# A hybrid decoder layer: the first three chunks side by side, and ten k-tiles of x transposed by blocks and a trip through DRAM

## The chip, the cores and the metric

The kernel runs on one core of a Trainium2 chip. The metric is the device time of one execution in microseconds. A core has five engines that work side by side, each with a queue of its own: TensorE (PE; its weight loads are shown as PEld), VectorE (DVE), ScalarE (ACT), GpSimd (POOL) and SyncE (SP), which here issues nearly all DMAs. An engine does its instructions in the order in which they stand; one that waits holds up all behind it.

## What is computed

One layer on x of 256 tokens by 2048, in float32: RMS-norm, one combined projection, two attention mixers, gates, an output projection, and an MLP.

```python
h = rms_norm(x, g_mix)
proj = h @ w_in                      # 2048 -> 11776: q, k, v of 12 + 8 heads, two gates
...                                  # dilated attention (12 heads), MoBA attention (8 heads)
mixed = jax.nn.sigmoid(g_a) * ya + jax.nn.sigmoid(g_b) * yb
x = x + mixed @ w_out
h2 = rms_norm(x, g_mlp)
x = x + jnp.square(jax.nn.relu(h2 @ w_up)) @ w_down
```

Here only the beginning matters: x is transposed, scaled by g_mix, and multiplied with w_in.

## The kernel before

**Slots.** All the large products are written as one list of 496 slots. A slot multiplies two k-tiles (2 x 128 rows) of a weight matrix, 512 columns wide (a chunk), with the 256 tokens. Float32 is done as three products of halves: `split` makes hi (ScalarE casts, line 150) and lo (VectorE subtracts, line 151) of the weights, and `split_tr` does the same for the transposed activations (lines 160, 161). A slot is 12 matmuls of 512 columns (lines 176 to 178): two k-tiles, two halves of the tokens, three products. w_in has 23 chunks of 8 slots each; before, chunk after chunk. A chunk's result is in two PSUM banks of tag acc, of which there are four.

**The loop.** At the end of the kernel a loop over j writes the program: the splits up to slot j + 2, the loads of weight pieces (1 MB, two slots each; `raw` has three buffers, hi and lo three each), then what the tables `at_dma`, `at_post` and `at_fill` hold for j, with the matmuls of slot j ahead of `at_fill`. For the slots in `EARLY`, `at_post` comes ahead of the splits. This sets only the order within each engine's queue. What stands at slot 16 in the code is not held back until then, unless it waits for something or stands behind something that waits.

**The start.** SyncE loads x in eight pieces and the first weight pieces in turn. TensorE does some warming transposes (line 655, 661), then transposes x: `x_fill(i)` (line 232) does two k-tiles with four transposes into two banks of tag fill, `x_post(i)` scales and splits them into `xT`. `x_fill(0)` stands ahead of slot 0, the other seven in and behind slots 0 to 5. GpSimd loads small gain vectors (lines 649, 652).

**A chunk's post work.** When a q or k chunk is done in slot j, `qk_done` puts into the tables: squares at j + 1 and j + 2, the scaling to `qn` at j + 3, 32 x 32 block transposes into `tq` at j + 4 (`blk`, line 210), four scatters of `tq` to DRAM at j + 6 (`wr`, line 215), one gather back at j + 8 (`rd`, line 220), the gain at j + 11. `tq` has one buffer. A scatter and a gather together complete the transposition; SyncE issues the gather only when the scatters have landed.

Of the kernel before, what the change touches and what calls it, by code (L numbers as in the profile page):

```python
# [76 lines left out]
def hybrid_block_kernel(ctx: ExitStack, tc: tile.TileContext, x, g_mix, w_in, q_norm_a, k_norm_a,  # L77
# [86 lines left out]
    def tok_major(banks, actT, k, first, last, hi, lo, between=None, cut=False):  # L164


        parts = [(0, 0, CW), (1, 0, CW)] if not cut else [(0, 0, CW), (1, 0, S), (1, S, CW)]
        order = [(i, kk) for i in range(len(parts)) for kk in range(2)]
        if between:
            order = [(i, kk) for kk in range(2) for i in range(2)]  # L170
        for i, (n, kk) in enumerate(order):
            t, a, b = parts[n]
            o = banks[t][:, a:b]
            s_hi = actT[:, k + kk, 0, t * P:(t + 1) * P]
            s_lo = actT[:, k + kk, 1, t * P:(t + 1) * P]
            nc.tensor.matmul(o, lhsT=s_hi, rhs=hi[:, kk, a:b], start=first and kk == 0, stop=False)  # L176
            nc.tensor.matmul(o, lhsT=s_hi, rhs=lo[:, kk, a:b], start=False, stop=False)  # L177
            nc.tensor.matmul(o, lhsT=s_lo, rhs=hi[:, kk, a:b], start=False, stop=last and kk == 1 and b == CW)  # L178
            if between and i == 1:
                between()  # L180

    def tok_chunk(src, k0, nk, c0, actT, ka, done):
# [584 lines left out]
```

## Time and profile before

| | |
|---|---|
| median of 3 runs | 1394.58 us (1394.02 to 1395.3) |
| the profiled execution | 1394.08 us, its span 1392.3 us |
| TensorE busy | 1385.7 us of the span |
| VectorE, ScalarE, GpSimd busy | 805.4, 649.1, 30.0 us |
| DMA | 317.67 MB, 228 GB/s on average |
| chain that ended last | 99% TensorE, 1% DMA |

The chain that ended last is followed back from the last instruction, at each step to what released it. A row of the timeline says when an instruction started, how long it took, its engine, line and operation, what it wrote and read, and in brackets how long the engine had been idle and what ended that. Rows with x4 stand for four instructions in a row; the time is that of all.

### The profile page before, as it was taken

The numbers are of one execution on the slowest core, as the hardware profiler recorded it, in microseconds if no ns is written. First come the engines' busy times: TensorE is split into PE (matmuls) and PEld (weight loads), VectorE is DVE, ScalarE is ACT, GpSimd is POOL, SyncE is SP. The second block draws the span as 40 slices with busy tenths as digits, with TensorE's granted clock in tenths as the row PEclk, the third lists the DMA queues.
The fourth block names the chain that finished last, engine by engine and source line by source line (L and its number), as shares of the span: only waits on it lengthen the run. The fifth ranks groups of instructions, "written<-read, shape, count | busy, mean of one in ns | idle before, by whom it ended". The sixth has DMA issues, their size and how long they took to land.

```text
span 1392.3 us, 16021 instructions
## 1 busy us (share of the span) xinstructions
PE 1385.7 (100%) x6168; PEld 1148.6 (83%) x6168; DVE 805.4 (58%) x951; ACT 649.1 (47%) x924; POOL 30.0 (2%) x49
## 2 busy tenths in 40 slices
PE   9999999999999999999999999999999999999998
PEld 7888888888888888888888888888888888888887
DVE  5666546666555544776657566544445656654443
ACT  6554445454444464444545445433334544543332
POOL 1101000010000000000000000000000000000000
PEclk9999999999999999999999999999999999999999
DMA  8777986778566655777878777665567787766562
GB/s 273 234 251 223 291 269 222 241 262 271 188 212 213 219 195 185 254 257 269 275 216 259 251 237 246 213 206 185 194 198 214 228 253 235 248 214 220 202 208 95
DMA packets 193027, 317.67 MB, mean 228 GB/s; under 512 B 8360, under 2 KB 54840, under 8 KB 192952
## 3 DMA queue, kind: packets, MB, share of 16 engines
q1 hardware_dynamic: 192664, 316.65, 70.0%
q8 instruction: 48, 0.79, 0.2%
q14 instruction: 27, 0.22, 0.0%
q0 software_dynamic: 256, 0.01, 0.0%
q10 hardware_dynamic: 32, 0.01, 0.0%
HBM read 288.85 MB, written 27.79 MB: 227 GB/s over the span
## 4 chain that ended last, share of the span: by engine, by line
PE 99%; DMA 1%; SPq 0%; DVE 0%; ACT 0%; issue 0%; DVEq 0%
PE acc L178 28%; PE acc L177 28%; PE acc L176 28%; PE fill L177 4%; PE fill L176 4%; PE fill L178 4%; PE fill L395 1%; PE fill L442 1%; DMA raw<-in_w_in_dram 1%; PE fill L394 0%; PE fill L444 0%; SPq L139 0%; PE fill L232 0%; SPq L224 0%; DVE lo L151 0%; ACT hi L150 0%
## 5 line engine op out<-in xcount | busy, mean ns | idle before, releaser
L151 DVE TENSOR_TENSOR lo<-raw,hi 128x1024 fp32r<-128x1024 f32 (+1 forms) x498 | 606.2, 1219 | 565.3 <-ACT hi L150 564.2
L150 ACT CAST hi<-raw 128x1024 fp32r<-128x1024 f32 (+1 forms) x498 | 523.0, 1051 | 688.5 <-PE acc L178 576.0
L176 PE MATMUL acc<-hi,xT 128*128 128x512 f32 x736 | 289.2, 393 | 0.0
L177 PE MATMUL acc<-lo,xT 128*128 128x512 f32 x736 | 286.7, 390 | 0.4 <-DVE lo L151 0.4
L178 PE MATMUL acc<-hi,xT 128*128 128x512 f32 x736 | 286.8, 390 | 0.0
L176 PE MATMUL acc<-hi,x1T 128*128 128x512 f32 x512 | 199.2, 389 | 0.0
L177 PE MATMUL acc<-lo,x1T 128*128 128x512 f32 x512 | 199.2, 389 | 0.0
L178 PE MATMUL acc<-hi,x1T 128*128 128x512 f32 x512 | 199.2, 389 | 0.0
L177 PEld LDWEIGHTS acc<-lo,xT 128*128 128x128 f32 x736 | 138.2, 188 | 29.7 <-DVE lo L151 1.1
L178 PEld LDWEIGHTS acc<-hi,xT 128*128 128x128 f32 x736 | 138.1, 188 | 29.2 <-DVE xT L161 0.5
L176 PEld LDWEIGHTS acc<-hi,xT 128*128 128x128 f32 x736 | 138.3, 188 | 28.3
L176 PEld LDWEIGHTS acc<-hi,x1T 128*128 128x128 f32 x512 | 96.1, 188 | 20.1
L177 PEld LDWEIGHTS acc<-lo,x1T 128*128 128x128 f32 x512 | 96.1, 188 | 19.9
L178 PEld LDWEIGHTS acc<-hi,x1T 128*128 128x128 f32 x512 | 96.1, 188 | 19.9
L177 PE MATMUL fill<-lo,h 128*128 128x512 f32 (+1 forms) x258 | 99.9, 387 | 0.0
L178 PE MATMUL fill<-hi,h 128*128 128x512 f32 (+1 forms) x258 | 99.9, 387 | 0.0
L176 PE MATMUL fill<-hi,h 128*128 128x512 f32 (+1 forms) x258 | 99.9, 387 | 0.0
L176 PE MATMUL acc<-hi,h 128*128 128x512 f32 x256 | 99.6, 389 | 0.0
L177 PE MATMUL acc<-lo,h 128*128 128x512 f32 x256 | 99.6, 389 | 0.0
L178 PE MATMUL acc<-hi,h 128*128 128x512 f32 x256 | 99.6, 389 | 0.0
L176 PEld LDWEIGHTS fill<-hi,h 128*128 128x128 f32 x258 | 48.4, 188 | 10.0
L178 PEld LDWEIGHTS fill<-hi,h 128*128 128x128 f32 x258 | 48.4, 188 | 9.9
(118 smaller groups left out, 1069.1 us busy)
## 6 DMA issues: line engine op xcount, KB each, us to landing
raw<-in_w_in_dram SPq DMA_DIRECT2D x89, 1024.0 KB, 5.8
raw<-in_w_up_dram SPq DMA_DIRECT2D x64, 1024.0 KB, 5.8
raw<-in_w_down_dram SPq DMA_DIRECT2D x64, 1024.0 KB, 5.1
scr<-tq SPq DMA_DIRECT2D x136, 128.0 KB, 4.9
raw<-in_w_out_dram SPq DMA_DIRECT2D x16, 1024.0 KB, 5.4
st<-scr SPq DMA_DIRECT2D x29, 512.0 KB, 5.6
raw<-in_w_branch_b_dram SPq DMA_DIRECT2D x8, 1024.0 KB, 5.2
raw<-in_w_branch_a_dram SPq DMA_DIRECT2D x4, 1024.0 KB, 5.0
```

The source lines that it names most:

```text
L150: nc.scalar.copy(hi[:, o], t[:, o])
L151: nc.vector.tensor_tensor(lo[:, o], t[:, o], hi[:, o].bitcast(F32), op=ALU.subtract)
L176: nc.tensor.matmul(o, lhsT=s_hi, rhs=hi[:, kk, a:b], start=first and kk == 0, stop=False)
L177: nc.tensor.matmul(o, lhsT=s_hi, rhs=lo[:, kk, a:b], start=False, stop=False)
L178: nc.tensor.matmul(o, lhsT=s_lo, rhs=hi[:, kk, a:b], start=False, stop=last and kk == 1 and b == CW)
L395: nc.tensor.matmul(b[:, P:P + S], lhsT=q[:, 1], rhs=k, start=True, stop=True)
L442: nc.tensor.matmul(st["o"][:, o:o + S], lhsT=v[:, 0, h * HD:(h + 1) * HD], rhs=pt[:, 0:2], start=(g == 0 or not joint), stop=False)
```

## The change

- **Side by side.** The first 24 slots take the chunks 0, 1 and 2 in turn, two k-tiles at a time (`stream_beside`): slot 0 is chunk 0 with k-tiles 0 and 1, slot 1 chunk 1 with the same, slot 2 chunk 2, slot 3 chunk 0 with k-tiles 2 and 3. A weight piece holds two such halves and is loaded by two DMAs. Chunks 2 and 3 use banks of tag fill. Chunks 0, 1 and 2 end in slots 21, 22 and 23, and their post work is shifted by 0, 3 and 6 slots.
- **Bounces.** K-tiles 0 to 5 of x are still transposed by TensorE. K-tiles 6 to 10 and 11 to 15 go through `x_bounce`: block transposes on VectorE (slots 2 and 5), four scatters to DRAM (3 and 6), one gather (5 and 9), scaling and splitting (7 and 12). x is loaded in five pieces.
- **Order of matmuls.** In slot 0 the products go k-tile by k-tile, first those with the hi half of the weights; `split(1)` works on both k-tiles at once.
- **Small loads.** The gain loads stand at slot 16, what uses them at 26; the sums of squares of x at 9 to 15.

```diff
-EARLY = (1, 2, 3, 4, 5, 6)
+EARLY = (1, 2, 5, 7)
...
+    def stream_beside(src, nk, c0, mains):
+
+        turns = [(a, i) for a in range(0, nk, 2) for i in range(len(mains))]
+        for n in range(0, len(turns), 2):
+            aps = [(2 * h, 2 * h + 2, src[a * P:(a + 2) * P, c0 + i * CW:c0 + (i + 1) * CW].rearrange(
+                "(k p) c -> p k c", p=P)) for h, (a, i) in enumerate(turns[n:n + 2])]
+            for h, (a, i) in enumerate(turns[n:n + 2]):
+                slots.append((aps, 2 * h, a, mains[i]))
...
+        if order == "start":
+            for kk in range(2):
+                for i in (0, 2, 1):
+                    for t in range(2):
+                        product(t, kk, 0, CW, i)
+            return
...
+    def x_bounce(u, k0, n, steps):
+
+        tq = T["xs"][:, u, 0].rearrange("p (t j f) -> p t j f", t=2, j=4)
+        st = T["xs"][:, u, 1].rearrange("p (t f) -> p t f", t=2)
+        scr = dp.tile([2, 4, 32, 4, 32 * n], F32, name=f"scrx{u}")
...
+        on(at_post, steps[0], blk)
+        on(at_dma, steps[1], lambda: scatter(scr, tq))
+        on(at_dma, steps[2], lambda: gather(st, scr))
+        on(at_post, steps[3], post)
...
-    def qk_done(kind, nh_off):
+    def qk_done(kind, nh_off, later=0):
 
         def done(banks, j):
+            j += later
...
-            done = qk_done("aq" if c < 3 else "ak", 4 * c)
+            done = qk_done("aq" if c < 3 else "ak", 4 * c, (0, 3, 6)[c] if c < 3 else 0)
...
+        if c < 3:
+            beside.append(tok_main(KD, lambda: T["xT"], 0, done, "fill" if c == 2 else "acc"))
+            if c == 2:
+                stream_beside(w_in, KD, 0, beside)
+        else:
+            tok_chunk(w_in, 0, KD, c * CW, lambda: T["xT"], 0, done, "fill" if c == 3 else "acc")()
...
-    x_post(0, b0)
-    split(0)
-
-    def mid():
-        split(1)
-        x_post(1, x_fill(1))
-        split(2)
-        load_all(3)
-        x_load(7)
-
-    T["mid"] = mid
-    for i in range(2, 8):
+    x_post(0, b0, (0,))
+    split(0, lambda: x_post(0, b0, (1,)))
+    split(1)
+    for i in (1, 2):
         st = {}
-        on(at_fill, i - 2, lambda i=i, st=st: st.update(b=x_fill(i)))
-        on(at_post, i - 1, lambda i=i, st=st: x_post(i, st["b"]))
-    on(at_post, 9, gain_post)
+        on(at_fill, i - 1, lambda i=i, st=st: st.update(b=x_fill(i)))
+        on(at_post, i, lambda i=i, st=st: x_post(i, st["b"]))
+    x_bounce(0, 6, 5, (2, 3, 5, 7))
+    x_bounce(1, 11, 5, (5, 6, 9, 12))
+    on(at_post, 16, gain_load)
+    on(at_post, 26, gain_post)
```

Three places show how the order in the queues moves. In all of them the name behind "waits" is a semaphore: DMAHW is one of the eight that SyncE's loads use in turn, so waiting for it is waiting for a DMA to land; DVE, Activation and Pool are engines.

The first is GpSimd's queue at the start; `half` is a constant, `grow` and `gn` take the gains, `sx` and `rstd` belong to the norm of x. Before, it stands so:

```order
L614 MEMSET half 128x8
L647 MEMSET grow_83 128x32
L649 DMA grow_83<-in_g_mlp_dram 16x32 [waits Pool_49]
L649 DMA grow_83<-in_g_mlp_dram 16x32 x3
L652 DMA gn<-in_q_norm_a_dram 128x1
L652 DMA gn<-in_k_norm_a_dram 128x1
L652 DMA gn<-in_q_norm_b_dram 128x1
L652 DMA gn<-in_k_norm_b_dram 128x1
L249 TENSOR_SCALAR vx<-sx 128x2 [waits DVE_49]
L250 TENSOR_TENSOR rstd<-vx,half 128x2 [waits Activation_49,Pool_49]
```

The small loads stand right behind the constants. After, GpSimd's queue begins so:

```order
L663 MEMSET half 128x8
L399 MEMSET rel_t 128x32
L691 MEMSET grow_83 128x32
L693 DMA grow_83<-in_g_mlp_dram 16x32 [waits Pool_49]
L693 DMA grow_83<-in_g_mlp_dram 16x32 x3
L696 DMA gn<-in_q_norm_a_dram 128x1
L696 DMA gn<-in_k_norm_a_dram 128x1
L696 DMA gn<-in_q_norm_b_dram 128x1
L696 DMA gn<-in_k_norm_b_dram 128x1
L290 TENSOR_SCALAR vx<-sx 128x2 [waits DVE_49]
L291 TENSOR_TENSOR rstd<-vx,half 128x2 [waits Activation_49,Pool_49]
```

The loads are the same rows at the same place; a memset of `rel_t` stands ahead of them now, and the only wait ahead of `sx` is for GpSimd's own memset.

The second is SyncE's queue in the opening. `raw` are the weight pieces, `xs` is the buffer of the bounces and `scrx0` the first one's DRAM. Before, from weight piece 3 on, it stands so:

```order
L139 DMA raw_197<-in_w_in_dram 128x4x512 [waits DMAHW0_49,DVE_49]
L224 DMA x_101<-in_x_dram 128x2x256 [waits DMAHW1_49]
L139 DMA raw_224<-in_w_in_dram 128x4x512 [waits DMAHW2_49,DVE_49]
L139 DMA raw_282<-in_w_in_dram 128x4x512 [waits DMAHW4_49,DMAHW6_49,DMAHW3_49,DVE_49]
L139 DMA raw_340<-in_w_in_dram 128x4x512 [waits DMAHW0_49,DVE_49]
L139 DMA raw_388<-in_w_in_dram 128x4x512 [waits DMAHW5_49,DMAHW2_49,DVE_49]
```

There is nothing but weights behind the last load of x, for six pieces. After, SyncE's queue from weight piece 4 on stands so:

```order
L148 DMA raw_199<-in_w_in_dram 128x2x512 [waits DMAHW1_49,DMAHW0_49,DVE_49]
L148 DMA raw_199<-in_w_in_dram 128x2x512
L148 DMA raw_250<-in_w_in_dram 128x2x512 [waits DMAHW3_49,DMAHW4_49,DMAHW2_49,DVE_49]
L148 DMA raw_250<-in_w_in_dram 128x2x512
L233 DMA scrx0_162<-xs_103 32x8x160
L233 DMA scrx0_162<-xs_103 32x8x160 [waits DMAHW5_49]
L233 DMA scrx0_162<-xs_103 32x8x160 [waits DMAHW6_49]
L233 DMA scrx0_162<-xs_103 32x8x160 [waits DMAHW7_49]
L148 DMA raw_291<-in_w_in_dram 128x2x512 [waits DMAHW0_49,DVE_49]
L148 DMA raw_291<-in_w_in_dram 128x2x512 [waits DMAHW1_49]
L238 DMA xs_103<-scrx0_162 128x2x640 [waits DMAHW6_49,DMAHW5_49,DMAHW7_49,DMAHW4_49,DMAHW2_49]
L233 DMA scrx1_163<-xs_103 32x8x160 [waits DMAHW3_49]
```

Between the weight pieces 5 and 6 stand the four scatters of the first bounce; the gather stands behind piece 6 and waits for the scatters (and all that is behind it waits too).

The third is VectorE's queue at the post work of chunks: `qn` is the scaled chunk, `tq` its block-transposed form, `lo` the lo halves of the weights for the next slots. Before, around chunk 3, it stands so:

```order
L278 TENSOR_TENSOR qn_1014<-acc_794,rrq_994 128x512 [waits Pool_49]
L278 TENSOR_TENSOR qn_1016<-acc_795,rrq_994 128x512
L151 TENSOR_TENSOR lo_1031<-raw_900,hi_1030 128x1024 [waits Activation_49]
L210 STREAM_TRANSPOSE tq_1036<-qn_1014 128x4x4x32 [waits DMAHW2_49,DMAHW1_49,DMAHW3_49,DMAHW0_49,DVE_49]
L210 STREAM_TRANSPOSE tq_1036<-qn_1016 128x4x4x32 [waits DVE_49]
L151 TENSOR_TENSOR lo_1052<-raw_939,hi_1051 128x1024 [waits DMAHW4_49,Activation_49]
L151 TENSOR_TENSOR lo_1068<-raw_939,hi_1067 128x1024 [waits Activation_49]
L151 TENSOR_TENSOR lo_1091<-raw_983,hi_1090 128x1024 [waits DMAHW6_49,Activation_49]
L151 TENSOR_TENSOR lo_1107<-raw_983,hi_1106 128x1024 [waits Activation_49]
```

The scatters for which tq_1036 waits were those of chunk 2, eight slots ahead. After, VectorE's queue at chunks 2 and 3 stands so; lo_956 is that of slot 35, lo_990 of 36, lo_1010 of 37 and lo_1036 of 38:

```order
L161 TENSOR_TENSOR lo_956<-raw_797,hi_955 128x1024 [waits Activation_49]
L228 STREAM_TRANSPOSE tq_963<-qn_932 128x4x4x32 [waits DMAHW6_49,DMAHW5_49,DMAHW7_49,DMAHW4_49,DVE_49]
L228 STREAM_TRANSPOSE tq_963<-qn_934 128x4x4x32 [waits DVE_49]
L161 TENSOR_TENSOR lo_990<-raw_851,hi_989 128x1024 [waits DMAHW1_49,Activation_49]
L320 TENSOR_TENSOR qn_993<-fill_734,rrq_975 128x512 [waits Pool_49]
L320 TENSOR_TENSOR qn_995<-fill_735,rrq_975 128x512
L161 TENSOR_TENSOR lo_1010<-raw_851,hi_1009 128x1024 [waits Activation_49]
L228 STREAM_TRANSPOSE tq_1020<-qn_993 128x4x4x32 [waits DMAHW5_49,DMAHW4_49,DMAHW6_49,DMAHW3_49,DVE_49]
L228 STREAM_TRANSPOSE tq_1020<-qn_995 128x4x4x32 [waits DVE_49]
L161 TENSOR_TENSOR lo_1036<-raw_895,hi_1035 128x1024 [waits Activation_49]
```

Two pairs of block transposes that were eight slots apart are two slots apart. The second pair waits for four DMAs, and these are the scatters of the first. In SyncE's queue at the same place they stand behind a weight piece that waits for lo_1010:

```order
L238 DMA st_961<-scr_897 128x2x512 [waits DMAHW5_49,DMAHW6_49,DMAHW4_49,DMAHW7_49,DMAHW2_49,DMAHW1_49]
L148 DMA raw_1013<-in_w_in_dram 128x4x512 [waits DVE_49]
L233 DMA scr_1015<-tq_963 32x8x128 [waits DMAHW3_49]
L233 DMA scr_1015<-tq_963 32x8x128 x3
L148 DMA raw_1057<-in_w_in_dram 128x4x512 [waits DVE_49]
L238 DMA st_1059<-scr_1015 128x2x512 [waits DMAHW4_49,DMAHW5_49,DMAHW3_49,DMAHW6_49,DMAHW1_49,DMAHW0_49]
L233 DMA scr_1061<-tq_1020 32x8x128
```

A gather and one weight piece follow them, and then the scatters of chunk 3. Before, SyncE's queue from the scatters of chunk 2 (scr_902) to those of chunk 3 (scr_1073) stood so:

```order
L215 DMA scr_902<-tq_865 32x8x128 x4
L139 DMA raw_939<-in_w_in_dram 128x4x512 [waits DMAHW5_49,DMAHW4_49,DVE_49]
L220 DMA st_941<-scr_902 128x2x512 [waits DMAHW2_49,DMAHW3_49,DMAHW1_49,DMAHW0_49]
L139 DMA raw_983<-in_w_in_dram 128x4x512 [waits DMAHW6_49,DVE_49]
L139 DMA raw_1034<-in_w_in_dram 128x4x512 [waits DMAHW7_49,DVE_49]
L139 DMA raw_1071<-in_w_in_dram 128x4x512 [waits DMAHW4_49,DVE_49]
L215 DMA scr_1073<-tq_1036 32x8x128 x4
```

Four weight pieces and a gather lay between a chunk's scatters and the next chunk's; after, one weight piece and a gather do.

## Rows read from the trace of the kernel before

**Rows 1.** The page, chain that ended last: share of each engine.

```profile
PE 99%; DMA 1%; SPq 0%; DVE 0%; ACT 0%; issue 0%; DVEq 0%
```

**Rows 2.** Waits of TensorE, whole span: who for whom: us in total, times, longest.

```profile
PE acc L177 <- DVE lo L151: 0.4, 1, 0.4
```

**Rows 3.** Chain in order of time, 15 to 36 us: start, us, what.

```profile
18.11 0.44 PE fill L232 x4
```

**Rows 4.** Timeline, TensorE, opening and slots 8 and 9: start, us, instruction, idle before.

```profile
1.35 2.39 PE L655 MATMUL acc<-ident 128*128 128x128 f32 x10 [1.35 <-POOL half L614]
...
6.15 0.78 PE L176 MATMUL acc<-hi,xT 128*128 128x512 f32 x1
...
33.49 0.39 PE L176 MATMUL acc<-hi,xT 128*128 128x512 f32 x1
...
36.22 0.39 PE L176 MATMUL acc<-hi,xT 128*128 128x512 f32 x1
```

**Rows 5.** Timeline, opening: casts and lo halves of slots 1 and 2.

```profile
8.97 1.30 ACT L150 CAST hi<-raw 128x512 fp32r<-128x512 f32 x2 [2.43 <-DMA raw<-in_w_in_dram]
...
12.79 1.05 ACT L150 CAST hi<-raw 128x1024 fp32r<-128x1024 f32 x1 [1.78 <-DMA raw<-in_w_in_dram]
...
13.87 1.23 DVE L151 TENSOR_TENSOR lo<-raw,hi 128x1024 fp32r<-128x1024 f32 x1 [2.09 <-ACT hi L150]
...
15.01 0.87 DVE L161 SCALAR_TENSOR_TENSOR xT<-fill,gT,xT 128x256 fp32r<-128x256 f32 x2
...
15.15 0.50 PE L177 MATMUL acc<-lo,xT 128*128 128x512 f32 x1 [0.39 <-DVE lo L151]
```

**Rows 6.** Timeline of VectorE and ScalarE, and one group by shape: steps of post work.

```profile
63.12 0.87 DVE L307 TENSOR_SCALAR qkva<-st,gqk 128x512 f32<-128x512 f32 x2
63.92 1.28 DVE L278 TENSOR_TENSOR qn<-acc,rrq 128x512 f32<-128x512 f32 x2
...
66.25 1.29 DVE L210 STREAM_TRANSPOSE tq<-qn 128x512 f32<-128x512 f32 x2
...
662.74 1.71 ACT L160 ACTIVATE x1T<-st,gT 128x256 fp32r<-128x256 f32 x4 [0.28 <-DMA st<-scr]
...
L210 DVE STREAM_TRANSPOSE ts<-s 128x768 f32<-128x768 f32 x4 | 3.9, 969 | 0.0
```

**Rows 7.** Timeline of SyncE's issues: weights (raw), scatters (scr), gathers (st).

```profile
49.63 0.37 SPq L139 DMA_DIRECT2D raw<-in_w_in_dram  x1
50.05 2.67 SPq L215 DMA_DIRECT2D scr<-tq  x4
...
56.93 0.38 SPq L220 DMA_DIRECT2D st<-scr  x1
...
73.41 0.37 SPq L139 DMA_DIRECT2D raw<-in_w_in_dram  x1
...
82.05 0.38 SPq L220 DMA_DIRECT2D st<-scr  x1
```

**Rows 8.** DMAs by tile, whole span: first the scatters' (scr), then the gathers' (st).

```profile
DMA to landing us min/median/max: 2.8/5.1/9.8
...
DMA to landing us min/median/max: 3.7/5.6/6.7
```

**Rows 9.** Timeline of VectorE, w_up: two chunks two slots apart.

```profile
741.86 1.31 DVE L210 STREAM_TRANSPOSE tq<-u 128x512 f32<-128x512 f32 x2 [1.98 <-DMA scr<-tq]
```

**Rows 10.** Timeline of GpSimd.

```profile
1.72 2.18 POOL L649 DMA_DIRECT2D grow<-in_g_mlp_dram  x4 [0.31 <-POOL grow L647]
...
41.45 0.12 POOL L357 MEMSET rel_t<- 128x32 f32 x1
```

**Rows 11.** Windows: us, busy (x instructions) by engine, granted clock, DMA share, GB/s.

```profile
6.00:10.00 4.00, 3.80 (x18) 2.67 (x17) 1.71 (x4) 1.52 (x4) 0.05 (x1) 1.00 0.81 283
10.00:14.00 4.00, 3.99 (x21) 2.86 (x20) 1.91 (x5) 2.22 (x5) 0.00 (x0) 1.00 0.93 333
14.00:20.00 6.00, 5.62 (x27) 4.24 (x26) 5.12 (x8) 6.00 (x15) 0.00 (x0) 1.00 1.06 375
```

More of the change, by code (lines that the diff above doesn't have):

```diff
@@ L134, in load_w @@
         t = wp.tile([P, 4, CW], F32, name="raw")
-        ap = slots[2 * piece][0]
-        n = 4 // parts
         raw[piece] = t
-        for i in range(parts):
-            yield lambda i=i: nc.sync.dma_start(out=t[:, i * n:(i + 1) * n], in_=ap[:, i * n:(i + 1) * n])
+        for a, b, ap in slots[2 * piece][0]:
+            n = (b - a) // parts
+            for i in range(parts):
+                yield lambda i=i, a=a, n=n, ap=ap: nc.sync.dma_start(out=t[:, a + i * n:a + (i + 1) * n],
+                                                                     in_=ap[:, i * n:(i + 1) * n])
     def load_all(piece):
@@ L148, in split @@
         lo = wp.tile([P, 2, CW], F32R, name="lo")
-        for o in ((slice(0, 1), slice(1, 2)) if j < 2 else (slice(0, 2),)):
+        for o in ((slice(0, 1), slice(1, 2)) if j == 0 else (slice(0, 2),)):
             nc.scalar.copy(hi[:, o], t[:, o])
             nc.vector.tensor_tensor(lo[:, o], t[:, o], hi[:, o].bitcast(F32), op=ALU.subtract)
+            if between and o.start == 0:
+                between()
         split_t[j] = (hi, lo)
@@ L162, in split_tr, with tok_major, product, tok_main @@
                                            op1=ALU.subtract)
[L164 to L182, printed above, removed]
+    def tok_major(banks, actT, k, first, last, hi, lo, order=None):
+        def product(t, kk, a, b, i):
+            nc.tensor.matmul(banks[t][:, a:b], lhsT=actT[:, k + kk, i // 2, t * P:(t + 1) * P],
+                             rhs=(hi, lo)[i % 2][:, kk, a:b], start=first and kk == 0 and i == 0,
+                             stop=last and kk == 1 and i == 2 and b == CW)
+        if order == "start":
[4 more added lines that the diff above has]
+            return
+        for t, a, b in [(0, 0, CW), (1, 0, S), (1, S, CW)] if order == "end" else [(0, 0, CW), (1, 0, CW)]:
+            for kk in range(2):
+                for i in range(3):
+                    product(t, kk, a, b, i)
+    def tok_main(nk, actT, ka, done, tag="acc"):
         st = {}
@@ L187, in main, with tok_chunk @@
             if k == 0:
-                st["b"] = [bank("acc") for _ in range(2)]
-            tok_major(st["b"], actT(), ka + k, k == 0, k + 2 == nk, hi, lo, T.get("mid") if j == 0 else None)
+                st["b"] = [bank(tag) for _ in range(2)]
+            tok_major(st["b"], actT(), ka + k, k == 0, k + 2 == nk, hi, lo, "start" if j == 0 else None)
             if k + 2 == nk:
                 done(st["b"], j)
+        return main
+    def tok_chunk(src, k0, nk, c0, actT, ka, done, tag="acc"):
+        main = tok_main(nk, actT, ka, done, tag)
         return lambda *p: stream(src, k0, nk, c0, main, p)
@@ L562, in main @@
                 end = part == 1 and k == 14
-                tok_major(st["b"], T[f"h{part}"], k, part == 0 and k == 0, end, hi, lo, cut=hf and c == 3 and end)
+                tok_major(st["b"], T[f"h{part}"], k, part == 0 and k == 0, end, hi, lo,
+                          "end" if hf and c == 3 and end else None)
                 if part == 1 and k == 14:
```

65 lines of the change are left out of this document (37 added, 28 removed).

## The prediction

> **What bounds the kernel now.** I read the chain that ended last first: 99% of it is TensorE [rows 1], and the only DMA on it is the wait for the first weights. Then TensorE's waits over the whole span: behind the opening there is one named wait, of 0.4 us [rows 2]. Then the timeline of TensorE: its work is cut into slots of twelve matmuls, and slot 8 starts at 33.49, slot 9 at 36.22, so a slot is 2.73 us, 0.2275 a matmul [rows 4], and so it goes to the end. The kernel is a gapless stream behind a rough opening. Whatever is taken out of the stream, or any hole made in it, moves the end by as much, since nothing later has slack to give it back. The DMA engines and VectorE matter only where they make TensorE run dry; hi and lo have three buffers, so TensorE can run at most about three slots past a VectorE that stands still.
>
> **Removed: transposes.** A group of four transposes costs the stream 0.44 us [rows 3]. Eight groups become three, the first of which lies ahead of the matmuls before and after. 5 x 0.44 = **-2.2 us**.
>
> **The opening.** Up to 6.15 us nothing moves: seven warming transposes run until then either way [rows 4]. Before, slot 9 starts at 36.22; nine slots (24.57) and seven groups (3.08) from 6.15 give 33.80, so 2.42 us were waits and slow matmuls. After, in the same way: slot 0 has no waits in its new order and ends at about 9.2; transposes until 9.65. Slot 1 is chunk 1 now and needs the third and fourth weight loads, which stand at the same place in the queue as before. The fourth lands at 9.66 (the second of the two casts at 8.97, 8.97 + 1.30 less one cast of some 0.6) [rows 5]. A whole cast now stands behind it: lo starts 1.08 after hi and TensorE's lo matmul 1.28 after lo [rows 5], so the second matmul is at 12.02, the slot ends at 14.52, transposes at 14.96. Slot 2 writes two banks that still hold transposed k-tiles 2 and 3; VectorE reads the first of them from 15.01 on [rows 5], some 0.5 us long, so slot 2 starts at 15.55. Seven slots and 0.09 behind transposes: slot 9 could start at 34.75. Waits have grown from 2.42 to 3.15: **+0.7**. If that were all, the end would come 1.5 us earlier.
>
> **The small loads do not move.** The order shows why: GpSimd has nothing that makes it wait ahead of them, so the place in the code at slot 16 holds nothing back. The trace has the same thing: rel_t's memset, written for slot 14 (about 50 us), ran at 41.45, as soon as GpSimd was done with the row ahead of it [rows 10]. I cost this edit at nothing, and take all landings of the opening from the trace of before, in which the loads leave from 1.72 on [rows 10]. From 6 to 10 us the DMA engines move 283 GB/s, from 14 on 375 [rows 11].
>
> **The first bounce, and slot 9.** K-tiles 6 and 7 are due in slot 9. VectorE's queue: lo of slot 2 starts at 13.87, as before, since its weight load lands at 12.79 either way [rows 5]. Then, by steps: lo 1.14, two passes over xT 0.89, lo 1.14, two passes 0.88, two block transposes of 640 columns at 0.81 (1.29 for two of 512, 0.97 for one of 768 [rows 6]), lo 1.14, lo of slot 5 1.23: 21.9. SyncE holds weight piece 5 until that lo is done, and the scatter stands behind it. Before, from a weight issue to the gather that waits for the scatter behind it are 7.3 us (49.63 to 56.93) and 8.6 (73.41 to 82.05) [rows 7]; here two half pieces are issued, with the end of x and two weight pieces still queued ahead, so I take 8.5: gather issued at 30.4. A gather lands 3.7 to 6.7 us after its issue, median 5.6 [rows 8]; I take 4.8, as the next piece ahead of it was issued at 27 already: 35.2. Behind it ScalarE, which has the five k-tiles ahead of slot 9's cast in its queue, needs 5 x 0.40 [rows 6], then 1.08 to lo and 1.28 to TensorE: 39.6 to 39.7. The second matmul of slot 9 would be due at 34.98. **+4.7** (bounds 3.6 and 6.6, from landings of 3.7 and 6.7).
>
> The second bounce is due in slot 15, at about 55.8; by the same steps its gather is issued near 43 and lands near 48.5. It costs nothing; its cover is 7 us, less 4.5 of passes and casts.
>
> **The tq buffer, and slot 38.** Chunks 0, 1 and 2 end in slots 21, 22 and 23, and their post work is put off by 0, 3 and 6 slots, chunk 3's is not. So the transposes of chunk 2 stand at slot 33, its scatter at 35, and the transposes of chunk 3 at 35 too. tq has one buffer: VectorE must wait for a scatter that SyncE issues in the very same slot, behind a weight load that itself waits for VectorE's lo of slot 37. Before, eight slots lay between two such chunks and VectorE was not held up here. The nearest row is late in the kernel, with two chunks two slots apart but the scatter one slot sooner: 1.98 us of waiting [rows 9]. Here the round trip is all there is. Counted from the start of slot 35: lo of slot 37 normally ends 2.4 in; VectorE carries a backlog (passes of 0.87 and 1.28 and blocks of 1.29 [rows 6], and a wait of about 1.5 for chunk 1's scatter in slot 33), so I take 3.6. Then 7.25 to the landing, as in [rows 7], then blocks 1.22, then 1.28 from lo of slot 38 to TensorE: 13.4. That matmul is due 8.4 after the start. **+5.0** (bounds 1.8, with no backlog and a trip of 5.2, which is the 2.4 to the last of the four issues and the quickest landing of 2.8 [rows 7, 8]; and 7.7, with 8.6 for this trip and for chunk 1's). Queued behind the waiting VectorE are the lo of slots 38 and 39; TensorE has eaten its three buffers by then.
>
> **The clock.** Two gaps of 4 to 5 us are longer than any that this trace has behind the opening, where the granted clock reads 1.00 [rows 11]. In the opening, from 1.35 to about 7 us, TensorE went at half pace: ten transposes in 2.39 [rows 4], against four in 0.44 [rows 3]. If a gap brings that back once, 5.5 us at half pace cost 2.75; if never, nothing. The nearest row of a gap, 0.4 [rows 2], speaks for nothing, but is far shorter. I take half of one such fall, **+1.4**, and 0 to 5.5 as bounds. [...]
>
> **Sum.** -2.2 + 0.7 + 4.7 + 5.0 + 1.4 = +9.6 us. The profiled execution of before took 1394.08 (span 1392.3), so 1403.7; the median of the runs is 0.5 above it: **1404.2 us**.
>
> **Rivals.**
> - Neither bounce is felt. Place: the gather's landing in the opening, and chunk 2's scatter. For: a scatter's DMA has landed in 2.8 us and a gather in 3.7 [rows 8]. Against: SyncE issues both behind weights that wait for VectorE, and two round trips are needed. It decides from the point where the gather lands by 30.6 and the scatter within 2.3 us of the lo ahead of it. Then -2.2 + 0.7 = -1.5 on the median of 1394.6: 1393.1, not slower. 0.06.
> - Only slot 9 waits, since the scatter of chunk 2 is issued or lands sooner than its place in the order says: -1.5 + 4.7 = +3.2: 1397.8. 0.08.
> - The small loads do wait for slot 16. From 6 to 14 us the DMA engines fell 92 and 42 GB/s short of their later 375 [rows 11], 0.54 MB or 1.4 us of loading; lo of slot 2, and with it the gather, comes that much sooner: +8.2: 1402.8 for the median, inside the forecast's band. 0.08. [...]
> - Both gaps bring the low clock back: -2.2 + 0.7 + 4.7 + 5.0 + 5.5 = +13.7: 1408.3. 0.15. [...]
> - Forecast: 0.63, from 1400 to 1407: its terms' bounds add up to +3.9 and +18.3, but not all stand at one end.
>
> **Range and chances.** 1398.5 to 1408.5 leaves out the first rival, most of the second and about half of the clock rival, 0.19. A measurement of this kernel tells 0.2%, 2.8 us, from no change. Faster by more: half of the first rival, 0.03. Within: its other half, 0.05 of the second, and 0.02 of the forecast's low tail, 0.10. Slower: 0.87.
>
> **What would show it.** GpSimd's loads from about 1.8 us on, not at 50. The second matmul of slot 1 near 12.0, and of slot 9 near 39.7, with ScalarE's cast released by the gather's landing. In slot 35 VectorE idle for about 7 us until scr<-tq, and a hole of about 5 us in TensorE near 119 us. TensorE's steps of 0.23 right behind both holes say that the clock stayed; steps near 0.43 that it fell. Wrong would be: no wait of VectorE for scr<-tq, a gather landed before 31, or holes elsewhere, as in slot 15.

## Result, and the profile after

The changed kernel takes 1407.76 us (median; 1407.28 to 1409.94), the kernel before 1394.30 beside it: ratio 1.0099, 95% interval 1.0087 to 1.0111, slower by 13.5 us. The forecast was 1404.2, with a range from 1398.5 to 1408.5. The profiled execution took 1407.28 us (span 1405.4), 13.2 more than the one of before.

In the chain that ended last, TensorE has fallen from the 99% of [rows 1] to 93%; what is new in it are the scatters' DMAs, VectorE and SyncE.

```profile
PE 93%; DMA 1%; DVE 1%; SPq 1%; issue 0%; ACT 0%; DVEq 0%
```

Most of this lies between 90.57 and 125.54 us, where the chain runs through the scatters of chunks 0, 1 and 2, one behind the other (start, us, what). TensorE was busy for most of these 35 us too, so its share of the chain fell by more than the 0.9% of the time that was lost.

```profile
95.32 4.76 DMA scr<-tq
...
106.05 4.99 DMA scr<-tq
...
118.50 4.46 DMA scr<-tq
```

Where the 13.2 us arose is seen by setting the start of the same slot in both traces side by side (us; "2nd" is a slot's second matmul):

| | before | after | later by | new in this stretch |
|---|---|---|---|---|
| slot 8 | 33.49 | 30.83 | -2.67 | -2.67, opening |
| slot 9, 2nd | 36.44 | 39.59 | 3.15 | +5.8, hole |
| slot 10 | 38.94 | 44.13 | 5.20 | +2.05, slow matmuls |
| slot 38, 2nd | 115.32 | 125.54 | 10.22 | +5.02, hole |
| slot 39 | 117.81 | 129.76 | 11.94 | +1.72, slow matmuls |
| slot 261 | 748.24 | 760.97 | 12.73 | +0.79, mostly at slot 228 |
| end of the span | 1392.27 | 1405.43 | 13.15 | +0.42, after the last matmul |

Before, both places ran without a gap. These are the second matmuls of slots 9 and 38 in the timeline of TensorE, each 0.23 behind its first, and the block transposes of chunk 3 in that of VectorE, which waited for nothing:

```profile
36.44 0.39 PE L177 MATMUL acc<-lo,xT 128*128 128x512 f32 x1
...
115.32 0.39 PE L177 MATMUL acc<-lo,xT 128*128 128x512 f32 x1
...
109.77 1.29 DVE L210 STREAM_TRANSPOSE tq<-qn 128x512 f32<-128x512 f32 x2
```

The two holes after, in the timeline of TensorE (start, us, instruction, idle before); the row at 33.32 is the last matmul of slot 8:

```profile
33.32 0.39 PE L180 MATMUL fill<-hi,xT 128*128 128x512 f32 x1
38.33 0.79 PE L180 MATMUL acc<-hi,xT 128*128 128x512 f32 x1 [4.62 <-ACT hi L160]
39.59 0.79 PE L180 MATMUL acc<-lo,xT 128*128 128x512 f32 x1 [0.47 <-DVE lo L161]
40.18 1.05 PE L180 MATMUL acc<-hi,xT 128*128 128x512 f32 x2
...
120.07 0.61 PE L180 MATMUL acc<-hi,xT 128*128 128x512 f32 x2
125.54 0.72 PE L180 MATMUL acc<-lo,xT 128*128 128x512 f32 x1 [4.86 <-DVE lo L161]
126.06 1.05 PE L180 MATMUL acc<-hi,xT 128*128 128x512 f32 x2
```

Behind each hole a pair of matmuls takes 1.05 us, against 0.61 ahead of it. It is the clock, as the windows show (us, busy (x instructions) of PE, PEld, DVE, ACT, POOL, granted clock, DMA share, GB/s):

```profile
33.00:38.00 5.00, 0.71 (x4) 0.25 (x2) 2.08 (x5) 2.76 (x6) 0.00 (x0) 0.89 0.67 220
38.00:44.00 6.00, 5.20 (x12) 3.78 (x13) 3.49 (x3) 3.41 (x7) 0.00 (x0) 0.52 0.56 177
44.00:50.00 6.00, 6.00 (x28) 4.97 (x27) 2.45 (x2) 3.57 (x7) 0.00 (x0) 1.00 0.80 282
121.00:125.60 4.60, 0.06 (x1) 0.06 (x1) 2.53 (x4) 0.54 (x1) 0.00 (x0) 1.00 0.32 95
125.60:129.00 3.40, 3.40 (x8) 2.67 (x9) 2.95 (x4) 0.00 (x0) 0.00 (x0) 0.51 0.18 17
129.00:135.00 6.00, 6.00 (x28) 4.92 (x27) 2.45 (x3) 3.37 (x10) 0.00 (x0) 0.99 0.99 326
```

TensorE is busy all through 125.60 to 129.00 and does 8 matmuls there, at a granted clock of 0.51; at the 0.23 us a step that it has at 1.00 there would be 15.

What the first hole waited for, in ScalarE's timeline: five passes over k-tiles, released by the landing of the gather (xs<-scrx), then the cast that slot 9 needs.

```profile
35.24 2.10 ACT L172 ACTIVATE xT<-xs,gT 128x256 fp32r<-128x256 f32 x5 [8.60 <-DMA xs<-scrx]
37.25 2.92 ACT L160 CAST hi<-raw 128x1024 fp32r<-128x1024 f32 x3
```

What the second waited for, VectorE and SyncE in one timeline: ahead of the block transposes of chunk 3 (123.07) VectorE stands idle for 7.17 us until the scatters of chunk 2, issued from 116.35 on, have landed; the lo half of slot 38 stands behind them. The row at 111.16 is the same conflict one chunk sooner: chunk 2 waits 1.55 us for the scatters of chunk 1.

```profile
111.16 1.31 DVE L228 STREAM_TRANSPOSE tq<-qn 128x512 f32<-128x512 f32 x2 [1.55 <-DMA scr<-tq]
...
114.69 1.21 DVE L161 TENSOR_TENSOR lo<-raw,hi 128x1024 fp32r<-128x1024 f32 x1
115.93 0.37 SPq L148 DMA_DIRECT2D raw<-in_w_in_dram  x1
116.35 2.66 SPq L233 DMA_DIRECT2D scr<-tq  x4
123.07 1.31 DVE L228 STREAM_TRANSPOSE tq<-qn 128x512 f32<-128x512 f32 x2 [7.17 <-DMA scr<-tq]
124.30 1.19 DVE L161 TENSOR_TENSOR lo<-raw,hi 128x1024 fp32r<-128x1024 f32 x1
```

GpSimd's small loads leave as early as in [rows 10]:

```profile
1.78 2.19 POOL L693 DMA_DIRECT2D grow<-in_g_mlp_dram  x4 [0.31 <-POOL grow L691]
```

### The profile page after: what moved, and what is told of

Its sections match the earlier page's. It is cut to its first block, busy times and chain, and to the rows that moved or that the text cites. A ratio compares the mean times of both kernels' runs of the same rounds, so it can differ in the third digit from the quotient of the medians.

```text
span 1405.4 us, 16002 instructions
## 1 busy us (share of the span) xinstructions
PE 1387.6 (99%) x6148; PEld 1149.3 (82%) x6148; DVE 808.0 (57%) x954; ACT 649.0 (46%) x923; POOL 29.7 (2%) x49
## 4 chain that ended last, share of the span: by engine, by line
PE 93%; DMA 1%; DVE 1%; SPq 1%; issue 0%; ACT 0%; DVEq 0%
PE acc L180 78%; PE fill L180 14%; DMA scr<-tq 1%; DVE lo L161 1%; PE fill L437 1%; PE fill L484 1%; SPq L233 0%; DVE tq L228 0%; PE fill L436 0%; PE fill L486 0%; ACT hi L160 0%; DVE qn L320 0%; ACT xT L172 0%; SPq L148 0%; DVE x L615 0%
## 5 line engine op out<-in xcount | busy, mean ns | idle before, releaser
L180 PE MATMUL acc<-hi,xT 128*128 128x512 f32 x1344 | 421.5, 393 | 4.6 <-ACT hi L160 4.6
L180 PE MATMUL acc<-hi,x1T 128*128 128x512 f32 x1024 | 315.7, 389 | 0.0
L180 PE MATMUL fill<-hi,h 128*128 128x512 f32 (+1 forms) x516 | 158.1, 387 | 0.0
L180 PEld LDWEIGHTS acc<-hi,h 128*128 128x128 f32 x512 | 96.1, 188 | 19.9
L180 PE MATMUL acc<-hi,mT 128*128 128x512 f32 x256 | 79.0, 389 | 0.0
L180 PE MATMUL acc<-hi,yT 128*128 128x512 f32 x192 | 59.3, 389 | 0.0
L180 PEld LDWEIGHTS fill<-lo,h 128*128 128x128 f32 x258 | 48.4, 188 | 10.0
L180 PEld LDWEIGHTS acc<-lo,h 128*128 128x128 f32 x256 | 48.0, 188 | 10.1
L180 PEld LDWEIGHTS acc<-hi,mT 128*128 128x128 f32 x256 | 48.1, 188 | 9.9
L180 PE MATMUL acc<-lo,mT 128*128 128x512 f32 x128 | 49.9, 390 | 0.4 <-DVE lo L161 0.4
```

Of the source, the lines that this page charges most:

```text
L180: nc.tensor.matmul(banks[t][:, a:b], lhsT=actT[:, k + kk, i // 2, t * P:(t + 1) * P], rhs=(hi, lo)[i % 2][:, kk, a:b], start=first and kk ...
```

## The experiments

Each kernel is the changed one with the edit shown; small lines that an edit needs besides are left out. The theory: the two holes and the low clock behind them are the whole loss; the first comes from the gather's place behind weight pieces, the second from the one tq buffer. Medians, and ratios to the kernel before (1394.2 to 1394.3 beside all of them):

| kernel | us | ratio, 95% interval |
|---|---|---|
| e1: second buffer for chunks 1 and 3 | 1401.47 | 1.0052, 1.0037 to 1.0067 |
| e2: scatter and gather sooner | 1403.45 | 1.0066, 1.0051 to 1.0081 |
| e3: holes filled with transposes | 1404.52 | 1.0082, 1.0062 to 1.0101 |
| e4: no bounces | 1403.15 | 1.0063, 1.0048 to 1.0078 |
| e5: small loads really late | 1406.15 | 1.0087, 1.0071 to 1.0102 |
| e6: both holes taken away | 1395.97 | 1.0010, 1.0001 to 1.0019 |
| e8: e4 and e1 | 1395.20 | 1.0006, 0.9997 to 1.0015 |
| e9: e6, slot 2's banks, e5 | 1394.07 | 0.9999, 0.9990 to 1.0008 |
| e10: e9, x cut at k-tile 12 | 1394.69 | 0.9999, 0.9990 to 1.0008 |
| e11: e10, second buffers later on | 1392.70 | 0.9992, 0.9983 to 1.0000 |
| e12: e11, order in slot 1 | 1391.57 | 0.9981, 0.9972 to 0.9989 |
| e13: e12, six useless transposes | 1391.83 | 0.9982, 0.9973 to 0.9991 |

**The tq buffer (e1).**

```diff
+                if spare:
+                    tq = T["xs"][:, 0, 0, 0:2 * CW].rearrange("p (t j f) -> p t j f", t=2, j=4)
+                else:
+                    tq = ap_.tile([P, 2, 4, CW // 4], F32, name="tq")
...
```

Here `spare` is true for the chunks 1 and 3.

> The changed kernel with one difference: the block transposes of chunks 1 and 3 go into a part of the bounces' buffer that nothing uses any more by then, those of chunks 0 and 2 into tq as they do; so chunk 3 need not wait for the scatters of chunk 2. Nothing is left out. Theory (the single buffer makes the hole in slot 38): VectorE's wait of 7.2 us in slot 35 is gone, with it the 5.03 us of waiting behind slot 38's first matmul and the 1.72 us of half clock that followed; 1407.3 - 6.75 = about 1400.5, slot 39 near 123. Rival (another wait, such as the gather or the weight piece behind the scatters, comes last in its place): a hole of 2 us or more stays in slots 37 to 40, and the time is 1404 or more.

1401.47, 6.3 us less. The row of this kernel that answers to 123.07 above, in VectorE's timeline, waits for nothing:

```profile
115.15 1.29 DVE L228 STREAM_TRANSPOSE xs<-qn 128x512 f32<-128x512 f32 x2
```

Slot 38's second matmul runs 0.23 behind its first, and between 50 us and the end TensorE waits 0.5 us in all. The single buffer made the second hole, and nothing took its place. The edit takes away chunk 2's wait for chunk 1 (1.55 us) together with chunk 3's wait for chunk 2 (7.17); what each is worth alone it does not tell. Of the 1 us above the expected 1400.5, 0.6 is there at slot 10 already (44.70, in the changed kernel 44.13): the opening differs, not the edit.

**The first bounce's place (e2).**

```diff
-    x_bounce(0, 6, 5, (2, 3, 5, 7))
+    x_bounce(0, 6, 5, (2, 2, 4, 7))
```

> The changed kernel with the first bounce's scatters one step and its gather one step sooner in SyncE's queue, so that the scatters stand ahead of weight piece 5 and the gather ahead of piece 6; nothing is left out. Theory (the place behind weight pieces that wait for VectorE sets the first bounce): the scatters leave about 18.2 instead of 22, the gather leaves about 27.5 instead of 30.6 and lands about 32 instead of 35.2, and slot 9's second matmul is at about 36.5 instead of 39.6; the hole of 4.8 us is 1.7, and the 2.05 us of half clock may go too: 1402 to 1404. Rival (the DMA engines' backlog sets it, the scatters queue behind the last of x and the weights in any order): landing at 35 as before, time 1407.

1403.45. In SyncE's timeline the scatters leave at 18.39 and the gather at 27.66:

```profile
18.39 1.82 SPq L233 DMA_DIRECT2D scrx<-xs  x4
...
27.66 0.37 SPq L238 DMA_DIRECT2D xs<-scrx  x1
```

Slot 9's second matmul is at 36.23 (TensorE's timeline), 3.4 sooner, and its steps are 0.23:

```profile
34.97 0.49 PE L180 MATMUL acc<-hi,xT 128*128 128x512 f32 x1 [0.97 <-ACT hi L160]
36.23 0.50 PE L180 MATMUL acc<-lo,xT 128*128 128x512 f32 x1 [0.77 <-DVE lo L161]
36.57 0.62 PE L180 MATMUL acc<-hi,xT 128*128 128x512 f32 x2
```

So the place in the queue decides, not the backlog alone. The low clock is gone from slot 9: the window from 33 to 39 us reads 1.00, and so does that from 38 to 44. Of the 5.3 us gained by the start of slot 10, 2.2 were lost again at slot 38. Chunk 2's block transposes now waited 2.92 us for the scatters of chunk 1, not 1.55 (VectorE's timeline), and the hole grew by 1.5 us; and the half clock there lasted longer (from 120.44 to 127.27, where the changed kernel had 125.65 to 129.07). A gain in the first hole is therefore not kept in full while tq has one buffer.

```profile
107.25 1.31 DVE L228 STREAM_TRANSPOSE tq<-qn 128x512 f32<-128x512 f32 x2 [2.92 <-DMA scr<-tq]
```

**The clock (e3).**

```diff
+    on(at_fill, 8, lambda: busy(T["spare"]["b"][0], 40))
+    on(at_fill, 37, lambda: busy(bank(), 40))
```

`busy(b, 40)` transposes the identity 40 times into the bank b.

> The changed kernel with work added that does nothing useful: 40 transposes of the identity on TensorE between slots 8 and 9 and 40 between slots 37 and 38, into banks whose contents are not wanted; at 0.11 us each they take 4.4 us, a little less than each of the holes (4.8 and 5.0). Nothing is left out. Theory (TensorE's idleness brought the low clock, and any work on it keeps the high one): the waits stay, but matmul steps behind both holes are 0.23 instead of 0.43, 2.05 + 1.72 = 3.8 us come back: 1403.5. Rival: the clock falls all the same, steps of 0.43 at both places, 1407 to 1408. [...]

1404.52, 3.2 us less, with work added. The transposes in the first hole (TensorE's timeline), and the windows over both:

```profile
34.59 4.53 PE L725 MATMUL fill<-ident 128*128 128x128 f32 x40
...
33.00:39.00 6.00, 6.00 (x49) 5.67 (x47) 2.83 (x6) 3.82 (x7) 0.00 (x0) 1.00 0.54 178
39.00:44.00 5.00, 4.83 (x23) 3.74 (x22) 3.30 (x4) 3.41 (x7) 0.00 (x0) 1.00 0.69 216
120.00:124.00 4.00, 3.08 (x28) 2.77 (x25) 2.17 (x3) 0.00 (x0) 0.00 (x0) 1.00 0.25 74
124.00:129.00 5.00, 4.71 (x21) 3.90 (x22) 4.10 (x6) 1.05 (x1) 0.00 (x0) 1.00 0.31 84
```

The clock stays at 1.00 through both places. Slot 9's second matmul is at 39.53 as before the edit: the wait is the same, only what follows it is faster. So it was idleness that brought the low clock (0.52 and 0.51 in the changed kernel's windows), and in this execution 40 float32 transposes in 4.53 us were enough, in each place, to hold the high one. Two new waits, which put off slots 65 and 69 by 0.56 and 0.76 us, took back part of the forecast 3.8: ScalarE's casts stood idle there for 5.16 and 5.38 us until weights had landed (193.17 and 204.83). Why these weights came late is not shown.

**Side by side without bounces (e4, e8).**

```diff
-    x_bounce(0, 6, 5, (2, 3, 5, 7))
-    x_bounce(1, 11, 5, (5, 6, 9, 12))
...
+    for i in range(3, 8):
+        on(at_fill, 3 * i - 4, lambda i=i: x_fill(i, spare["b"]))
+        on(at_post, 3 * i - 3, lambda i=i: x_post(i, spare["b"]))
```

> The changed kernel without the bounces: k-tiles 6 to 15 of x are transposed by TensorE in five groups of four between slots 5 and 17, chunks still side by side and chunk 3 still waiting for tq; nothing is left out. Theory (the first bounce makes the hole of slot 9, nothing else in the opening does): slots 9 and 10 run without a wait at full clock; slot 12 starts about 0.5 us sooner than in the kernel before, counting the groups passed by then; the hole of slot 38 and its half clock stay (6.75). 1394.3 - 0.5 + 6.75 = about 1400.5, 6.8 under the changed kernel. Rival (running the chunks side by side by itself starves slot 9, of weights or of VectorE): a hole of over 2 us near slots 9 to 12, and 1403 or more.

1403.15, 2.6 more than expected. The cause of the first hole is confirmed: TensorE runs slots 3 to 37 without a named wait. The expectation missed in two places. The other hole was larger:

```profile
121.89 0.79 PE L180 MATMUL acc<-lo,xT 128*128 128x512 f32 x1 [5.60 <-DVE lo L161]
```

The half clock lasted from 119.85 to 126.67, so that slot 38 cost 8.1 us, not 6.75; both waits for tq ahead of it were longer than in the changed kernel (1.94 and 7.52 against 1.55 and 7.17). And the opening gave less: slot 12 stood 0.3 ahead of the kernel before, where 0.5 was expected, and with the eighth group of transposes passed slot 19 started 0.81 later.

e8 has e1's edit as well.

> No bounces, all k-tiles of x transposed by TensorE, and chunk 3's block transposes in a buffer of their own; of the change only the chunks side by side and the moved small work remain. Nothing is left out. Theory (side by side alone gains nothing, since TensorE does the same work): slot 19 starts 0.8 us behind the kernel before, as it did with the bounces away and tq still single, and the hole at 38 is gone: 1394.3 + 0.8 = 1395.1, from 1394.3 to 1396. Rival (side by side saves waits of the opening by itself): 1393 or less.

1395.20: the hole is gone (slot 38's second matmul at 116.95, 0.23 behind its first), and what is left cannot be told from the kernel before. Setting chunks side by side gains nothing by itself here; it only puts off when k-tiles are needed. In the profiled execution, at 1395.98, slot 19 stood 1.6 behind the kernel before and not 0.8; in slot 1 TensorE had half clock there, of which more below.

**The small loads (e5).**

```diff
-    on(at_post, 16, gain_load)
+    on(at_post, 18, gain_load)
```

> The changed kernel with GpSimd's small loads put behind its work on the norm of x, which waits for VectorE: now they do leave late, near 65 us, and the opening is without them. Nothing is left out. Theory (they do slow the opening's loads, by the 283 against 375 GB/s of the windows, but only that): the loads of the first weights and of x land about 1.3 us sooner, slot 1 and slot 2 start sooner, and slot 9's second matmul is about 1.3 us sooner; the holes and the low clock stay; 1406. Rival (they cost nothing): landings within the spread of the openings seen so far (fourth weight load at 8.4 to 9.2 us), 1407.5.

1406.15; the intervals of this and the changed kernel overlap, so the time alone shows no gain. The rows do: behind `rstd`, which waits for VectorE, the loads leave at 65.14, and the DMA engines move more from 6 to 10 us. First the changed kernel's window, then this one's:

```profile
6.00:10.00 4.00, 4.00 (x20) 3.03 (x18) 1.84 (x4) 1.58 (x3) 0.12 (x1) 1.00 0.80 284
```

```profile
6.00:10.00 4.00, 4.00 (x19) 3.21 (x17) 1.47 (x3) 1.44 (x3) 0.00 (x0) 1.00 0.97 349
```

The first weights landed no sooner (the fourth load at 9.14, in the changed kernel at 8.37), against the expectation; the gather was issued at 28.98 instead of 30.63 and slot 9's second matmul came at 37.87 instead of 39.59.

**Both holes taken away (e6).**

```diff
...
+    on(at_fill, 5, lambda: x_fill(3, spare["b"]))
+    on(at_post, 6, lambda: x_post(3, spare["b"]))
-    x_bounce(0, 6, 5, (2, 3, 5, 7))
-    x_bounce(1, 11, 5, (5, 6, 9, 12))
+    x_bounce(0, 8, 4, (2, 3, 5, 10))
+    x_bounce(1, 12, 4, (5, 6, 9, 15))
```

> The changed kernel with chunk 3's block transposes in a buffer of their own (as in the experiment on tq) and with eight k-tiles on the way through DRAM instead of ten: 6 and 7 go by TensorE, so the first bounced k-tile is due in slot 12, 8.2 us later than in the changed kernel. Nothing is left out. Theory (the holes and the clock behind them are all that the change lost): no hole in slots 9 to 18 nor at 38; slot 9 starts 0.7 to 2.2 us sooner than in the kernel before, as the openings of the four kernels with bounces gave at slot 8 (2.7, 1.2, 2.4, 1.6 sooner) less 0.49 for one group of transposes; behind it up to 1 us of the late waits that some of these kernels had near slots 229 and 261; 1394.3 - 1.0 = 1393.3, from 1392 to 1394.5. Rival (something else in the side-by-side stretch still starves TensorE, such as ScalarE standing still for the gather): a hole of 1 us or more in slots 10 to 18, and 1396 or more.

1395.97: 11.8 us under the changed kernel, with no wait of TensorE in slots 9 to 38 and the clock at 1.00 from 6.57 on. So the holes and the clock are nearly all that the change lost. It missed the expected 1393.3 by 2.7 us. Half of that, 1.35 us, is a hole of this edit's own making, in slot 4: the four k-tiles 8 to 11 lie in two loads of x, so VectorE (its timeline) waited for the last one. Another 0.6 us are waits late in the kernel (e11 below), and 0.4 lie behind the last matmul.

```profile
20.29 1.30 DVE L228 STREAM_TRANSPOSE xs<-x 128x512 f32<-128x512 f32 x2 [2.43 <-DMA x<-in_x_dram]
```

**Towards a faster version (e9 to e13).** Each has the edits of the one ahead of it; e9 starts from e6.

e9, with e5's edit as well:

```diff
-        on(at_fill, i - 1, lambda i=i, st=st: st.update(b=x_fill(i)))
-        on(at_post, i, lambda i=i, st=st: x_post(i, st["b"]))
+        on(at_fill, (0, 2)[i - 1], lambda i=i, st=st: st.update(b=x_fill(i)))
+        on(at_post, (1, 3)[i - 1], lambda i=i, st=st: x_post(i, st["b"]))
```

> The kernel with eight bounced k-tiles and chunk 3's own buffer, and two further edits: the third group of transposes stands behind slot 2 instead of ahead of it, so that slot 2 finds two banks that are long free; and the small loads really wait, as in the experiment on them. Nothing is left out. Theory: slot 2's wait for VectorE's pass over xT (0.3 to 1.0 us in the runs so far) is gone and the opening's loads land about 1.3 us sooner, of which slot 1 gains some 0.8: 1391.8, from 1391 to 1393.5. Rival (the opening is bound by the landing of the weights of slots 1 and 2, whichever bank they write): as the kernel with eight bounced k-tiles, 1393.3.

1394.07, 1.9 us under e6: slot 2 started at 13.09 without a wait (15.60 in e6). It is not the expected 1391.8, since the wait for x had grown to 3.2 us and the hole of slot 4 stayed.

e10:

```diff
-    x_load(6, 5)
+    x_load(6, 6)
...
-    x_load(11, 5)
+    x_load(12, 4)
```

> The last kernel (eight bounced k-tiles, a buffer of chunk 3's own, the third group of transposes behind slot 2, the small loads late) with x's last two loads cut at k-tile 12 instead of 11, so that the first bounce's four k-tiles, 8 to 11, come with one load. Nothing is left out. Theory (VectorE's wait of 3.2 us for the last of x, ahead of the lo halves of slot 4, makes the 1.4 us hole behind slot 4's first matmul): the block transposes start when the load of k-tiles 6 to 11 lands, near 14.3, and the hole is gone; 1394.1 - 1.4 = 1392.7. Rival (the weights of slot 4 come too late in any case): the hole stays, or moves by the 0.6 us by which the larger load puts them off, and the time is 1394 or more.

The block transposes started at 15.32 without a wait and the hole in slot 4 was gone, as the theory has it; the median was not lower (1394.69, runs from 1392.30 to 1395.45). In the profiled execution matmuls of slot 1 went at half pace:

```profile
11.80:15.20 3.40, 3.40 (x9) 2.63 (x8) 2.95 (x4) 2.10 (x4) 0.00 (x0) 0.50 1.04 393
```

The same stood in the profiled executions of e8 (12.31 to 15.72) and e11 (12.04 to 15.46), not in the others.

e11, in `bounce_chunk`:

```diff
-            st["tq"] = tq = ap_.tile([P, 2, 4, CW // 4], F32, name="tq")
+            st["tq"] = tq = T[spare] if spare else ap_.tile([P, 2, 4, CW // 4], F32, name="tq")
...
```

> As the kernel before it in this study, and in the two places later on where two chunks end two slots apart (the first two of w_out, the first two of w_up) the second chunk's block transposes go into a buffer that is free there, not into tq. Nothing is left out. Theory (the waits near slots 229 and 261, up to 0.5 us each, are VectorE's waits for the first chunk's scatters, the same conflict over tq as at slot 38): no wait of TensorE near those slots, VectorE waits nowhere for scr<-tq; 0.5 us under the kernel before it in this study, 1392.2. Rival (they come from something else, such as weights landing late): waits of 0.3 us or more stay at slots 229 or 261, no difference.

1392.70, and from slot 6 to the last matmul every slot stands 0.7 ahead of the kernel before: the steps at slots 228 and 260 are gone. They were the same conflict over tq, at the chunks that end two slots apart, as in [rows 9]. In VectorE's timeline these block transposes, now into another buffer, wait for nothing:

```profile
654.50 1.30 DVE L228 STREAM_TRANSPOSE s<-x 128x512 f32<-128x512 f32 x2
...
739.05 1.30 DVE L228 STREAM_TRANSPOSE s<-u 128x512 f32<-128x512 f32 x2
```

e12:

```diff
-            tok_major(st["b"], actT(), ka + k, k == 0, k + 2 == nk, hi, lo, "start" if j == 0 else None)
+            tok_major(st["b"], actT(), ka + k, k == 0, k + 2 == nk, hi, lo, "start" if j < 2 else None)
```

> The last kernel (with a second buffer wherever two chunks end two slots apart) with one difference: slot 1 has its matmuls in the order of slot 0, four with the hi half of the weights ahead of the first with the lo half. Nothing is left out. Theory (the second matmul of slot 1 waits 1.0 us for VectorE's lo, while the matmuls with hi could run): three matmuls of 0.23 more stand ahead of that wait, so 0.7 us of it is hidden: 1392.7 - 0.7 = 1392.0, from 1391 to 1393, and where the clock does not fall back in slot 1, lower. Rival (slot 2 waits for its own weights, banks or clock as long): slot 2 starts no sooner, 1392.7.

**1391.57** (1391.31 to 1391.77): faster than the kernel before, by 0.11% to 0.28%. Slot 1 (TensorE's timeline) now has four matmuls ahead of the first lo, and no named wait:

```profile
10.06 1.20 PE L180 MATMUL acc<-hi,xT 128*128 128x512 f32 x4
11.32 0.73 PE L180 MATMUL acc<-lo,xT 128*128 128x512 f32 x2
11.89 1.09 PE L180 MATMUL acc<-hi,xT 128*128 128x512 f32 x4
```

From the start of slot 1 to that of slot 2 it took 3.21 us, against 3.82 in e9, which had no half clock there either: 0.6 of the forecast 0.7. How much of the 2.7 us under the kernel before is due to the change itself is not shown, since the kernel before was not run with late small loads and second buffers.

e13:

```diff
+    on(at_fill, 0, lambda: busy(b0[0], 6))
```

> The kernel before it in this study with six useless transposes of the identity on TensorE between slots 0 and 1, 0.66 us at 0.11 each, inside the gap of 1 us or more that is there. Nothing is left out. Theory (the half clock that the records show from about 12 to 15.5 us in three of the kernels, and not in the others, comes from the gaps of slots 0 to 2): with less idleness the records show no half clock in slot 1, and the runs, which for some kernels lie in two groups near 1392.5 and 1395, lie in the lower: 1391.8. Rival (the opening's clock does not go by this gap): some half clock in slot 1 still, or the two groups still, 1392 to 1393; if slot 1's weights land early, the transposes hold it up by up to 0.7 us.

1391.83. Neither e12 nor e13 showed half clock in slot 1, so this tells nothing of its cause. Slot 1 started at 11.06, 1.0 later than in e12; 0.6 of that arose in slot 0 already, ahead of the transposes, where the granted clock reached 1.00 at 8.13, in e12 at 6.84.

## Why the prediction was right or wrong

- **Sign and range: right.** The likeliest case, from 1400 to 1407, was passed by 0.8 us; what came true is the rival in which both gaps bring the low clock back (1408.3, given 0.15). That it lies 0.5 from the median is partly luck: its 5.5 for the clock was 1.7 too high, and waits of 1.2 that stood in no sum made up for most of it.
- **The small loads: right**, rows at 1.78 as said. What they cost when they do wait is near the forecast 1.4: 1.6 between the medians, with overlapping intervals, and 1.7 at slot 9's second matmul.
- **Slot 9: right in time.** Second matmul forecast 39.6 to 39.7, measured 39.59; gather issued 30.63 (30.4) and landed 35.22 (35.2). e4 shows that the bounce is the cause, e2 that its place behind the weight pieces is.
- **The opening: mis-sized.** -2.2 + 0.7 = -1.5 was forecast, -2.67 measured at slot 8. The second matmul of slot 1 stood at 10.81, not 12.02, since the fourth weight load landed at 8.37, not 9.66. Slot 2 started at 14.37, not 15.55: its weights landed at 11.59, where the trace of before was taken to hold (12.79). Other kernels with the same bounces had 14.60 to 15.83 there and -1.2 to -2.5 at slot 8, so a large part may be the spread of the first landings. It did not matter here: the gather sets slot 9's second matmul, and a sooner slot 8 only made the hole longer (5.8 instead of 4.7).
- **Slot 38: right, step by step.** A backlog of 3.8 from the start of slot 35 (112.13 to 115.90) against 3.6; 7.2 to the landing against 7.25; 13.41 in all against 13.4; a hole of 5.02 against 5.0. That it came out to a hundredth is luck with terms that were medians; that the buffer is the cause is shown by e1.
- **The clock: the step that failed.** Half of one fall, 1.4, stood in the sum; both holes brought the low clock, for 2.05 and 1.72, 3.8 in all. No row of before has a gap of this length, and the half was a mean between cases rather than a decision. A whole fall, priced at 2.75 by the opening's 5.5 us at half pace, was too dear: of the first half clock (36.91 to 43.73) 1.4 us lay in the hole itself, and the second lasted 3.41 us. In both holes of this trace what TensorE waited for stood behind a DMA's landing (the gather's at 35.22, the last scatter's at 122.96), and the work behind both ran at a granted clock of 0.52 and 0.51. That a gap brings the low clock back was an estimate of the author's until then; e3 shows that idleness is the cause here, since with transposes in the holes the clock read 1.00.
- **Late waits: not seen.** +0.79 from slot 39 to 261 and +0.42 after the last matmul were not in the sum. e11 shows that the first are again waits for scr<-tq; those of VectorE grew there from 0.74 and 1.98 us to 1.48 and 3.37. Row 741.86 of [rows 9] was used as a price for slot 38, but not as a wait that stands a fraction of a microsecond from reaching TensorE. The last 0.42 arose behind VectorE's last step, of which only the output's DMA is left: from that step to the end it took 4.6 us in the kernel before, 5.0 in this one and 4.7 to 5.0 in the others. Its cause is not shown.

The sum from these parts: 3.15 to slot 9's second matmul, 2.05, 5.02, 1.72, 0.79, 0.42 = 13.15, the difference of the two spans.

Still open is why slot 1 fell to half clock in some executions. The gap ahead of its second matmul does not decide it: that matmul stood at 11.63 in e6, without a fall, and at 11.50 in e10, with one.

## What to carry to other kernels

When work is interleaved, ask of every single-buffered intermediate how many slots now lie between two uses: a buffer that was safe at eight slots cost 6.3 us at two, and in two other places of the kernel before, with two slots between uses, VectorE had been waiting for it by up to 2 us, unnoticed. Such a conflict also takes back gains made ahead of it: the sooner TensorE came to slot 38 in e2, the longer it waited there. A transposition by way of DRAM is two round trips plus their places in the queue (here 14 us from the first scatter's issue to the gather's landing); it can pay only for tiles due later than that, so give the nearest tiles to TensorE. That it pays at all no run here shows: e6, with eight k-tiles on this way, took 1395.97, e8, with none, 1395.20. Price a hole of several microseconds in TensorE with the clock behind it included, here 2.05 and 1.72 us on holes of 5.8 and 5.0.
